# Gate and up projections of a SwiGLU: a fourth feature pair in seven products, and two pairs split by casting and adding DMAs

## The chip, the cores and the metric

The kernel runs on one core of one Trainium2 chip. The metric is the device time of one execution, in microseconds (us). The time before is 2090.59 us, the median of three runs (2089.03 to 2092.39).

## The reference

The reference is an encoder of two layers over 256 tokens of width 2048, in float32. Each layer mixes tokens (layer 0 by a gated spatial MLP, layer 1 by grouped-query attention), attends to 256 memory tokens, projects the joined heads and then runs a SwiGLU feed-forward network, which the change is about:

```
def swiglu(h, w_gate_up, w_down):
    gate, up = jnp.split(h @ w_gate_up, 2, axis=-1)
    return (jax.nn.silu(gate) * up) @ w_down

x = x + concatenate([tok_out, mem_out]) @ w_out[l]
x = x + swiglu(rms_norm(x, g_ffn[l]), w_gate_up[l], w_down[l])
```

`w_gate_up` is 2048 x 11264 (5632 gate and 5632 up columns), `w_down` 5632 x 2048.

## The kernel before, in words

Every matrix product is made of three: both operands are cut into a high part, rounded to the type float32r, and a low part, the rest, and hi x hi, lo x hi and hi x lo are accumulated in PSUM (`matmul3`, L193). The activations are cut once per layer. The weights are cut as they arrive: a DMA from SyncE's queue (SP) brings a `raw` tile of up to four 128x512 pieces, ScalarE casts it to `whi` (L248) and VectorE subtracts to get `wlo` (L249). There are three buffers each of `raw`, `whi` and `wlo` (`halves`, L244, and `W_TILES`, L35). A buffer of `whi` or `wlo` is given back when TensorE has used it; a `raw` buffer when VectorE has read it.

The feed-forward network of a layer works on 11 feature blocks of 512 gate and 512 up columns. A block is one `Pair` (L307). It walks over eight pairs of contraction chunks (2 x 128 rows each, index `i`), and each pair is a 2x2 block product: two chunks of the contraction by two token tiles on one side, two chunks by gate and up on the other. `eight` (L358) makes it in the ordinary eight products. `seven` (L340) makes it in seven, after Strassen and Winograd: VectorE first adds the four raw weight pieces to four sums `T` (L342 to L344), the three raw pieces that are used alone and the four sums are cut into halves, and the activations' sums come from `activation_sums` (L294), made once per layer for pairs 0 to 3 (`feature_sums`, L713). Of the pairs, 0, 1 and 2 are done in seven products and 3 to 7 in eight; the first block of a layer takes the five first, all the others the three first (L739).

The products land in PSUM banks by name: 1, 5, 6 and 7 in the pool `psm` (shared with all transposes), 2, 3, 4 and 8 in `psa`, four banks each. After the last pair in seven products `inner` (L367) combines 1, 5, 6 and 7 in five steps (one on ScalarE, four on VectorE), and at the block's end `outer` (L379) combines the rest in four VectorE steps. Then ScalarE takes the silu of the gate and VectorE multiplies it by up (L743, L744).

The order of the work is written in the program: `tick()` is called after every half unit of products and `later(n, fn)` puts a piece of work n ticks on. So a gate's output is transposed on TensorE and cut (`turn_a`, L731) some ticks after its block, among the products of the next one. Within the program's dependences a scheduler with a timeline model sets the order on each engine at build time; at run time each engine and each DMA queue takes its own list strictly in order.

The blocks come in chunks (L727: 4, 4 and 3 blocks). After each chunk `w_down` is applied to its outputs, in four column blocks of `Linear` (L252), and the result is added to `x` in SBUF (L753).

SBUF room: `room["p"]` is a pool that is opened for the mixing stage of a layer (36 tiles of 2 KB a partition), closed, and opened again for the feed-forward stage (24 such tiles, two `T` tiles of 8 KB, four of `e`). A new tile in it waits for the old tiles that lay in the same place. The pool `wp` (`raw`, `whi`, `wlo`) lives through the whole program.

Of the kernel before, what the change touches and what calls it, by code (L numbers as in the profile page):

```python
# [10 lines left out]
F32 = mybir.dt.float32  # L11
F32R = mybir.dt.float32r
# [21 lines left out]
FFN_TILES = 24  # L34
# [17 lines left out]
def encoder(ctx: ExitStack, tc: tile.TileContext, x, mem, g_mix, g_ffn, w_in_a, g_v_a, w_spatial, b_spatial,  # L52
# [190 lines left out]

    def halves(raw, n):  # L244

        hi = wp.tile([P, KC4, NB], F32R, tag="whi", name=nm("whi"))[:, :n]
        lo = wp.tile([P, KC4, NB], F32R, tag="wlo", name=nm("wlo"))[:, :n]
        nc.scalar.copy(hi, raw)  # L248
        nc.vector.tensor_tensor(lo, raw, hi.bitcast(F32), ALU.subtract)  # L249
        return [(hi[:, c, :], lo[:, c, :]) for c in range(n)]  # L250

    class Linear:  # L252
# [6 lines left out]
        def fetch(self, k0, n):  # L259
            raw = wp.tile([P, KC4, NB], F32, tag="raw", name=nm("raw"), bufs=3)  # L260
            src = self.w[k0 * P:(k0 + n) * P, self.n0:self.n0 + NB]
            nc.sync.dma_start(raw[:, :n], src.rearrange("(c p) n -> p c n", p=P))
            self.raw[k0] = raw
# [43 lines left out]
    class Pair:  # L307
# [3 lines left out]
        def __init__(self, parts, sums, w, na, nb, order, fast):  # L311
            self.parts, self.sums, self.w, self.na, self.nb = parts, sums, w, na, nb
            self.order, self.fast, self.bank, self.part = order, fast, {}, {}
            last = [i for i in order if i in fast][-1]
            rest = [i for i in order if i not in fast]
            for i in order:
                raw = self.fetch(i)
                (self.seven if i in fast else self.eight)(i, raw)
                if i == last:
                    self.inner()  # L320
            self.outer(bool(rest))

        def fetch(self, i):
            raw = wp.tile([P, KC4, NB], F32, tag="raw", name=nm("raw"), bufs=3)
            rows = slice(2 * i * P, (2 * i + 2) * P)
            for cut, n0 in ((slice(1, 3), self.na), (slice(0, 4, 3), self.nb)):
                nc.sync.dma_start(raw[:, cut], self.w[rows, n0:n0 + NB].rearrange("(c p) n -> p c n", p=P))
            return raw

        def add(self, name, a, b, i):  # L330
# [3 lines left out]
            some = len([x for x in self.order if x in self.fast])  # L334
            many = len(self.order) - some
            of = {1: some, 5: some, 6: some, 7: some, 8: 2 * many}.get(name, some + 2 * many)
            self.part[name] += 1
            matmul3(self.bank[name], a, b, self.part[name] == 1, self.part[name] == of)

        def seven(self, i, raw):  # L340
            T = room["p"].tile([P, KC4, NB], F32, tag="T", name=nm("T"), bufs=2)
# [11 lines left out]
            for some in (inner, outer):  # L353
                for name, a, b in some:
                    self.add(name, a, b, i)
                tick()

        def eight(self, i, raw):  # L358
            w01, w00, w10, w11 = halves(raw, 4)
            get, k0, k1 = self.parts.get, 2 * i, 2 * i + 1  # L360
            for t, names in ((0, (2, 3)), (1, (4, 8))):
                for name, pair in zip(names, ((w00, w10), (w01, w11))):
                    self.add(name, get(k0, t), pair[0], i)
                    self.add(name, get(k1, t), pair[1], i)
# [209 lines left out]
    for l in range(DEPTH):  # L574
        scope = ExitStack()
        room["p"] = scope.enter_context(tc.tile_pool(name=f"mix{l}", bufs=MIX_TILES, reuse_waits="tile"))
        cat = Parts()
        m = Memory(l)
        if l == 0:
# [28 lines left out]
            def gate(t, c):  # L608
# [4 lines left out]
                sb[t][c] = big()  # L613
# [95 lines left out]
        fast = [0, 1, 2]  # L709
        slow = [3, 4, 5, 6, 7]  # L710
        sums = {}

# [10 lines left out]
        later(4, lambda: feature_sums(1))  # L723
# [3 lines left out]
        chunks = [range(0, 4), range(4, 8), range(8, 11)]  # L727
        for chunk in chunks:
# [9 lines left out]
            for f in chunk:  # L738
                order = slow + fast if f == 0 else fast + slow  # L739
                g = Pair(hF, sums, w_gate_up[l], f * NB, DFF + f * NB, order, fast)  # L740
                for t in range(NT):
# [3 lines left out]
                    wait = 3 if f == chunk[-1] else 2 * len(fast) + 3  # L745
# [55 lines left out]
```

## Time and profile before

| what | before |
|---|---|
| median of three runs | 2090.59 us |
| the profiled execution, its own time | 2092.77 us |
| its span, first to last instruction | 2090.8 us |
| granted TensorE clock, mean | 0.991 |
| matmuls | 9346 |
| bytes moved by DMA | 396.01 MB, mean 189 GB/s |
| SP's DMA queue: packets' time as a share of 16 engines | 56.2% |

The span is shorter than the execution's own time by what lies before the first and after the last instruction. All durations in the prediction come from this one profiled execution. PE is TensorE, PEld its weight loads, DVE is VectorE, ACT ScalarE, POOL GpSimd and SP SyncE. In a group's row the first number after the bar is busy time in us, then the mean of one instruction in ns, and after the next bar the engine's idle time just before these instructions and what ended it.

### The profile page before, as it was taken

How to read it: one execution, taken by the hardware profiler on the slowest of the kernel's cores; microseconds unless marked ns; L12 is line 12 of the kernel's file. 1: busy time of each engine (PE TensorE's matmuls, PEld its weight loads, DVE VectorE, ACT ScalarE, POOL GpSimd, SP SyncE). 2: the span in 40 equal slices, each digit the busy share in tenths (PEclk: the TensorE clock that was granted, in tenths of full speed). 3: DMA queues.
4: the chain of work that ended last, by engine and by line, in shares of the span. 5: the costliest groups of instructions: out<-in, count | busy, mean ns of one | idle time of the engine just before them, and what ended most of it. 6: DMA issues, size and time to landing. Idle time of an engine off the chain costs nothing.

```text
span 2090.8 us, 23855 instructions
## 1 busy us (share of the span) xinstructions
PE 2052.3 (98%) x9346; PEld 1697.9 (81%) x9346; DVE 1485.8 (71%) x1502; ACT 1038.9 (50%) x1150; POOL 39.3 (2%) x50
## 2 busy tenths in 40 slices
PE   8799999899999999999999999998999999999999
PEld 6688888688888888888888878877888888888887
DVE  5466557987578875787567776688965889657964
ACT  7555444545344543445555654544543456434542
POOL 0010000000000000000000010000000000000000
PEclk9899999999999999999999999999999999999999
DMA  8655555465556555656556534545565655656564
GB/s 274 233 173 165 187 181 181 162 201 199 184 192 210 201 194 189 201 191 204 186 171 224 172 121 161 182 161 181 181 213 190 202 181 194 210 200 201 178 211 135
DMA packets 204696, 396.01 MB, mean 189 GB/s; under 512 B 9660, under 2 KB 12840, under 8 KB 204584
## 3 DMA queue, kind: packets, MB, share of 16 engines
q1 hardware_dynamic: 202432, 392.86, 56.2%
q10 hardware_dynamic: 2152, 1.63, 0.3%
q8 instruction: 73, 1.20, 0.2%
q14 instruction: 39, 0.32, 0.0%
HBM read 390.26 MB, written 4.19 MB: 189 GB/s over the span
## 4 chain that ended last, share of the span: by engine, by line
PE 92%; DVE 3%; issue 2%; DMA 2%; ACT 1%; SPq 0%; ACTq 0%; DVEq 0%
PE acc L195 27%; PE acc L196 27%; PE acc L197 27%; PE m L195 3%; PE m L196 3%; PE m L197 3%; PE m L201 2%; DVE wlo L249 1%; DMA a<-in_mem 1%; ACT whi L248 1%; PE m L473 0%; DVE T L342 0%; DMA gh_mq<-in_g_mq 0%; PE m L612 0%; DVE T L343 0%
## 5 line engine op out<-in xcount | busy, mean ns | idle before, releaser
L249 DVE TENSOR_TENSOR wlo<-raw,whi 128x2048 fp32r<-128x2048 f32 (+3 forms) x369 | 797.2, 2165 | 368.9 <-ACT whi L248 367.4
L248 ACT CAST whi<-raw 128x2048 fp32r<-128x2048 f32 (+3 forms) x369 | 666.5, 1812 | 646.0 <-PE acc L196 559.6
L195 PE MATMUL acc<-whi,h 128*128 128x512 f32 x1428 | 561.2, 394 | 10.1 <-DVE e L381 8.3
L196 PE MATMUL acc<-whi,h 128*128 128x512 f32 x1428 | 559.0, 392 | 0.0
L197 PE MATMUL acc<-wlo,h 128*128 128x512 f32 x1428 | 540.9, 392 | 0.0
L195 PE MATMUL acc<-whi,a 128*128 128x512 f32 x1154 | 451.5, 392 | 0.6 <-DVE a L404 0.6
L197 PE MATMUL acc<-wlo,a 128*128 128x512 f32 x1154 | 449.7, 391 | 0.0
L196 PE MATMUL acc<-whi,a 128*128 128x512 f32 x1154 | 449.5, 391 | 0.0
L195 PEld LDWEIGHTS acc<-whi,h 128*128 128x128 f32 x1428 | 270.0, 189 | 65.6 <-DVE e L381 9.1
L196 PEld LDWEIGHTS acc<-whi,h 128*128 128x128 f32 x1428 | 269.9, 189 | 55.2
L197 PEld LDWEIGHTS acc<-wlo,h 128*128 128x128 f32 x1428 | 268.7, 188 | 55.5 <-DVE wlo L249 0.4
L197 PEld LDWEIGHTS acc<-wlo,a 128*128 128x128 f32 x1154 | 217.1, 188 | 44.8
L195 PEld LDWEIGHTS acc<-whi,a 128*128 128x128 f32 x1154 | 217.2, 188 | 44.4 <-DVE a L404 0.8
L196 PEld LDWEIGHTS acc<-whi,a 128*128 128x128 f32 x1154 | 217.1, 188 | 44.0
L248 ACT CAST whi<-T 128x2048 fp32r<-128x2048 f32 x66 | 126.2, 1913 | 118.3 <-PE acc L196 110.6
L249 DVE TENSOR_TENSOR wlo<-T,whi 128x2048 fp32r<-128x2048 f32 x66 | 150.9, 2287 | 29.6 <-ACT whi L248 29.6
L342 DVE TENSOR_TENSOR T<-raw 128x1024 f32<-128x1024 f32 x66 | 80.4, 1218 | 18.7 <-DMA raw<-in_w_gate_up 18.7
L195 PE MATMUL m<-whi,a 128*128 128x512 f32 x198 | 80.0, 404 | 1.8 <-ACT whi L248 1.8
L196 PE MATMUL m<-whi,a 128*128 128x512 f32 x198 | 79.4, 401 | 0.0
L189 ACT CAST a<-m 128x512 fp32r<-128x512 f32 x80 | 46.3, 585 | 41.2 <-PE m L197 17.9
L190 DVE TENSOR_TENSOR a<-m,a 128x512 fp32r<-128x512 f32 x80 | 54.1, 684 | 17.0 <-ACT a L189 17.0
L197 PE MATMUL m<-wlo,a 128*128 128x512 f32 x198 | 55.9, 391 | 1.3 <-DVE wlo L249 1.3
(123 smaller groups left out, 1262.3 us busy)
## 6 DMA issues: line engine op xcount, KB each, us to landing
raw<-in_w_gate_up SPq DMA_DIRECT2D x352, 512.0 KB, 4.6
raw<-in_w_down SPq DMA_DIRECT2D x88, 1024.0 KB, 5.1
raw<-in_w_out SPq DMA_DIRECT2D x32, 1024.0 KB, 5.1
raw<-in_w_in_a SPq DMA_DIRECT2D x24, 1024.0 KB, 5.1
raw<-in_w_in_b SPq DMA_DIRECT2D x24, 1024.0 KB, 5.2
raw<-in_w_mem_kv SPq DMA_DIRECT2D x16, 1024.0 KB, 5.2
raw<-in_w_in_a SPq DMA_DIRECT2D x7, 512.0 KB, 5.8
x<-in_x SPq DMA_DIRECT2D x8, 256.0 KB, 4.7
```

Of the source, the lines that this page charges most:

```text
L189: nc.scalar.copy(hi, src)
L190: nc.vector.tensor_tensor(lo, src, hi.bitcast(F32), ALU.subtract)
L195: nc.tensor.matmul(out, lhsT=a[0], rhs=b[0], start=start, stop=False)
L196: nc.tensor.matmul(out, lhsT=a[1], rhs=b[0], start=False, stop=False)
L197: nc.tensor.matmul(out, lhsT=a[0], rhs=b[1], start=False, stop=stop)
L201: nc.tensor.transpose(dst[:, c * P:(c + 1) * P], src[:, c * P:(c + 1) * P], ident)
L248: nc.scalar.copy(hi, raw)
L249: nc.vector.tensor_tensor(lo, raw, hi.bitcast(F32), ALU.subtract)
L342: nc.vector.tensor_tensor(T[:, 0:2], raw[:, 1:4:2], raw[:, 0:1].to_broadcast([P, 2, NB]), ALU.add)
```

## The change

Four things are changed in the feed-forward stage:

- Pairs 0 to 3 are done in seven products, 4 to 7 in eight (before: 0 to 2, and 3 to 7). The sums for pair 3 were made before already; `feature_sums(1)` is put off from tick 4 to tick 6.
- Two of the four pairs in eight products get their halves from DMAs on GpSimd's queue (`laid`): one DMA casts the weights from float32 to float32r straight into `dhi`, ScalarE writes the negative of it into `dlo`, and a second DMA adds the weights onto that, which leaves the low half. Each of these DMAs brings 128 x 2 x 512 values (512 KB), for gate and then for up. There are three buffers each of `dhi` and `dlo`, in the pool of the feed-forward stage.
- The pairs are interleaved. In the strings F is a pair in seven products, S one in eight with halves from ScalarE and VectorE, D one in eight with halves from DMAs.
- The chunks are 3, 3, 3 and 2 blocks instead of 4, 4 and 3, and the waits before `turn_a` are set anew (15 ticks instead of 9; at the end of a chunk 3, or 1 for the chunk of two, instead of 3).

To make room, the feed-forward pool has 20 instead of 24 tiles and one `T` instead of two, `wp` has two `raw` buffers instead of three, the third one lying in the mixing stage's pool while that is open (`raw_tile`), and in layer 0 the gating result is written over `v` instead of into a tile of its own.

```
-FFN_TILES = 24
+FFN_TILES = 20
+LAID = 3
...
+    def raw_tile():
+        raws[0] += 1
+        pool = room["p"] if room["mixing"] and raws[0] % 3 == 0 else wp
+        return pool.tile([P, KC4, NB], F32, tag="raw", name=nm("raw"), bufs=1 if pool is not wp else 2)
...
+            for i, way in order:
+                if way == "D":
+                    self.laid(i)
+                else:
+                    raw = self.fetch(i)
+                    (self.seven if way == "F" else self.eight)(i, raw)
                 if i == last:
                     self.inner()
-            self.outer(bool(rest))
+            self.outer(many > 0)
+
+        def laid(self, i):
+            rows = slice(2 * i * P, (2 * i + 2) * P)
+            for n0, names in ((self.na, (2, 4)), (self.nb, (3, 8))):
+                src = self.w[rows, n0:n0 + NB].rearrange("(c p) n -> p c n", p=P)
+                hi = room["p"].tile([P, KC2, NB], F32R, tag="dhi", name=nm("dhi"), bufs=LAID)
+                lo = room["p"].tile([P, KC2, NB], F32R, tag="dlo", name=nm("dlo"), bufs=LAID)
+                nc.gpsimd.dma_start(hi, src)
+                nc.scalar.activation(lo, hi.bitcast(F32), AF.Copy, scale=-1.0)
+                nc.gpsimd.dma_start(lo, src, accum_op=ALU.add)
+                for t, name in enumerate(names):
+                    for c in range(KC2):
+                        self.add(name, self.parts.get(2 * i + c, t), (hi[:, c, :], lo[:, c, :]))
+                tick()
...
-            T = room["p"].tile([P, KC4, NB], F32, tag="T", name=nm("T"), bufs=2)
+            T = room["p"].tile([P, KC4, NB], F32, tag="T", name=nm("T"), bufs=1)
...
-                sb[t][c] = big()
+                sb[t][c] = v[t][c]
...
-        fast = [0, 1, 2]
-        slow = [3, 4, 5, 6, 7]
+        first = list(zip((4, 5, 0, 6, 1, 7, 2, 3), "DSFDFSFF"))
+        later_on = list(zip((0, 4, 1, 5, 2, 6, 3, 7), "FDFSFDFS"))
...
-        later(4, lambda: feature_sums(1))
+        later(6, lambda: feature_sums(1))
...
-        chunks = [range(0, 4), range(4, 8), range(8, 11)]
+        chunks = [range(0, 3), range(3, 6), range(6, 9), range(9, 11)]
...
-                order = slow + fast if f == 0 else fast + slow
-                g = Pair(hF, sums, w_gate_up[l], f * NB, DFF + f * NB, order, fast)
+                g = Pair(hF, sums, w_gate_up[l], f * NB, DFF + f * NB, later_on if f else first)
...
-                    wait = 3 if f == chunk[-1] else 2 * len(fast) + 3
+                    wait = 2 * len(chunk) - 3 if f == chunk[-1] else 15
```

34 lines of the change are left out of this document (17 added, 17 removed).

## The prediction

> **What bounds the kernel now.** I read the page first, then the chain of waits, the table by stretches, the list of waits, and the groups of instructions with their forms kept apart. From the page:
>
> ```profile
> span 2090.8 us, 23855 instructions
> ...
> PE 2052.3 (98%) x9346; PEld 1697.9 (81%) x9346; DVE 1485.8 (71%) x1502; ACT 1038.9 (50%) x1150; POOL 39.3 (2%) x50
> ...
> PE 92%; DVE 3%; issue 2%; DMA 2%; ACT 1%; SPq 0%; ACTq 0%; DVEq 0%
> ```
>
> TensorE carries the end: 92% of the chain that ended last is its own work. A busy figure of pipelined matmuls says little of their pace, so I take the pace from the chain in order of time, inside the gate/up stage of layer 0:
>
> ```profile
> 449.68 0.68 PE m L197 x3
> ...
> 492.10 0.68 PE m L197 x3
> ```
>
> Three matmuls of 512 columns take 0.68 us, 0.227 each (the mean of 392 ns that the page gives for one contains the overlap with the next). The two rows are the same product in neighbouring feature blocks: one block (a `Pair`, and its two gate outputs turned) takes 42.4 us. It has 3 x 7 + 5 x 8 = 61 products of three matmuls: 183 x 0.2267 = 41.5 us, and its eight transposes make up the rest. So TensorE has no hole there. The table by stretches, one such block, then the first block of layer 0:
>
> ```profile
> 437.00:479.40 42.40, 42.40 (x192) 35.12 (x192) 37.48 (x33) 22.24 (x16) 0.00 (x0) 1.00 0.59 198
> 350.00:392.00 42.00, 37.83 (x160) 30.85 (x159) 40.34 (x50) 22.09 (x20) 0.00 (x0) 0.96 0.45 150
> ```
>
> The columns are length, then PE, weight loads, VectorE (DVE), ScalarE (ACT), GpSimd (POOL) busy, granted clock, DMA share and GB/s. VectorE is busy 37.5 of 42.4 us, so it is close behind TensorE. In the first block it is the one that is late:
>
> ```profile
> PE acc L195 <- DVE e L381: 4.2, 1, 4.2
> PE m L197 <- DVE wlo L249: 1.7, 2, 1.1
> PE m L195 <- ACT whi L248: 0.7, 1, 0.7
> ```
>
> These are TensorE's waits from 340 to 410 us: 6.6 us in one layer, as three seven-product units follow each other at the block's end. So a gain comes from fewer matmuls, as long as VectorE, ScalarE and the DMAs stay ahead.
>
> **The change part by part.** Call a unit of two contraction chunks F (seven products), S (eight, split by ScalarE and VectorE) or D (eight, split by DMAs). Prices:
>
> ```profile
> L249 DVE TENSOR_TENSOR wlo<-raw,whi 128x2048 fp32r<-128x2048 f32 x294 | 671.7, 2290 | 362.6 <-ACT whi L248 362.1
> ...
> L248 ACT CAST whi<-raw 128x2048 fp32r<-128x2048 f32 x294 | 560.1, 1912 | 519.4 <-PE acc L196 448.0 <-issue 34.1 <-DMA raw<-in_w_gate_up 25.3
> ...
> L249 DVE TENSOR_TENSOR wlo<-T,whi 128x2048 fp32r<-128x2048 f32 x66 | 150.9, 2287 | 29.6 <-ACT whi L248 29.6
> L248 ACT CAST whi<-T 128x2048 fp32r<-128x2048 f32 x66 | 126.2, 1913 | 118.3 <-PE acc L196 110.6 <-DVE T L344 7.6
> L249 DVE TENSOR_TENSOR wlo<-raw,whi 128x1536 fp32r<-128x1536 f32 x66 | 115.6, 1751 | 1.4 <-ACT whi L248 0.4
> L248 ACT CAST whi<-raw 128x1536 fp32r<-128x1536 f32 x66 | 97.9, 1484 | 125.1 <-PE acc L196 111.6 <-issue 13.5
> L342 DVE TENSOR_TENSOR T<-raw 128x1024 f32<-128x1024 f32 x66 | 80.4, 1218 | 18.7 <-DMA raw<-in_w_gate_up 18.7
> ...
> L343 DVE TENSOR_TENSOR T<-T,raw 128x512 f32<-128x512 f32 x66 | 45.4, 687 | 1.2
> L344 DVE TENSOR_TENSOR T<-T,raw 128x512 f32<-128x512 f32 x66 | 45.2, 686 | 0.6
> ...
> L381 DVE TENSOR_TENSOR e<-acc,e 128x512 f32<-128x512 f32 x22 | 15.2, 690 | 57.1 <-PE acc L197 57.1
> ...
> L248 ACT CAST whi<-raw 128x1024 fp32r<-128x1024 f32 x7 | 7.3, 1048 | 1.4 <-DMA raw<-in_w_in_a 1.4
> ```
>
> *Products.* 4 x 7 + 4 x 8 = 60 instead of 61 per block: 22 blocks x 3 matmuls x 0.2267 = 15.0 us off the path itself. F lasts 21 x 0.2267 = 4.76 us on TensorE, S and D 5.44, a block 41.7.
>
> *VectorE and ScalarE.* F costs VectorE 1.218 + 0.687 + 0.686 + 1.751 + 2.287 = 6.63 us, S 2.29, D nothing. Per block one more F for an S is +4.34, two S turned to D are -4.58: -0.24, so about 37.2 of 41.7 us; still just under TensorE. ScalarE: F 3.40, S 1.91, D two negations of 128x1024. No such negation is in the trace; the cast of that size takes 1.05 and a cast of a quarter more than half of 1.91, so I take 1.05 each. That is 1.49 + 2 x 0.19 = +1.9, 24 of 41.7 us. Both are hidden by TensorE.
>
> *The order F D F S F D F S.* Before, three F in a row ask 19.9 us of VectorE in 14.3 of TensorE; now F and D ask 6.6 and F and S 8.9 in 10.2, which evens the load. Against it: the four combining steps of `inner` and, close behind, three of `outer` now lie behind the last F, with one S after it, not five. The tight place is from the moment that this F gives back its first split buffer (2.0 us into it) to the second split of the next block's first F: 2.7 + 5.4 + 0.9 (transposes) = 9.0 us. There VectorE has 1.75 + 2.29 + 7 x 0.69 = 8.9 us to do. I take no wait (VectorE idled 4.9 us in a block above, and TensorE waited for nothing); the other end is one output split more, 0.7 us late, x 22 = 15.
>
> *Raw buffers: three become two in the feed-forward stage.* Landing of a half tile (512 KB; two make a tile), as the DMA issues list it, with the spread that the view of the tensor gives:
>
> ```profile
> raw<-in_w_gate_up SPq DMA_DIRECT2D x352, 512.0 KB, 4.6
> ```
>
> ```profile
>   ACT whi L248: 25.3, 18
>   DVE T L342: 18.7, 14
> ...
> DMA to landing us min/median/max: 3.5/4.6/7.3
> ```
>
> The two upper rows are who waited for these tiles and how long; it cost TensorE nothing. The two halves are issued together, so a tile takes about 5.0. With two buffers the tightest tile is that of the next block's first F: its buffer is free when the last F's first split is done (3.2 us after the split buffer, which is free with the fourth unit at 20.4 us of the block): 23.6 + 5.0 + 2.6 for T = 31.2, and its own split buffer is free at 32.6. So 1.4 us of room before a late landing reaches VectorE. I take 0.
>
> *D units.* Each D is four 512 KB DMAs on GpSimd's queue (8 a block, 176 in all): cast into hi, negate on ScalarE, add into lo, for gate and then for up. GpSimd's queue is otherwise empty here (0.00 above). What queues behind the waits: the adding DMA waits for the negation and holds the next cast DMA on that queue; the negation waits for the cast DMA and holds ScalarE's casts behind it. No row shows a casting or adding DMA. Near end: two landings of 4.6 + 1.05 = 10.3 us; far end: the slowest row twice, 2 x 7.3 + 1.05 = 15.7. With three buffers each of hi and lo, the shortest stretch from release to use is from the middle of one D to the middle of the next: 2.72 + 4.76 + 5.44 + 4.76 + 2.72 = 20.4. Both ends fit, so I take 0; landings over (20.4 - 1.05)/2 = 9.7 do not fit.
>
> *The first D of each layer.* Now the layer starts with a D whose tiles lie where the mixing stage's pool lay. How early loading ran ahead before, and where TensorE's work starts:
>
> ```profile
> 313.55 29.59 SPq L327 DMA_DIRECT2D raw<-in_w_gate_up  x12
> ```
>
> ```profile
> 337.42 0.39 PE L195 MATMUL acc<-whi,h 128*128 128x512 f32 x1
> ```
>
> Raw tiles had their own pool and could start 24 us ahead. The D tiles wait for the mixing tiles under them, some of which the output projection may read to its end: 0 (all free 10 us ahead) to 10.3 us (none). I take 2 per layer, nearer the low end since only lo's place can be that late and it is wanted 4.6 us after hi's.
>
> *One more chunk end (3+3+3+2 for 4+4+3).* The same down products, eight more accumulations into x per layer on VectorE, which has room in the down stage; TensorE waits at no chunk end now. The last block of the two-block chunk is turned after one step of 2.7 us, when its gate is ready by the combining steps above: 0, at most 1 per layer. `sb` in place, pool sizes and the third raw tile in the mixing pool keep three raw tiles there: 0.
>
> *First block of a layer.* D S F D F S F F ends in S F F instead of F F F; the 6.6 us of waits may shrink or, with `inner` still behind the last F, stay: I take 0.
>
> Sum: the profiled run's own 2092.77 - 15.0 + 2 x 2 = 2081.8; the median of the three runs, 2090.59, lies 2.2 below it: **2079.6**. With the first D between 0 and 2 x 4.6 and up to 6 us fewer first-block waits, this case lies between 2069 and 2086.
>
> **The rivals.**
>
> *Late landings (slower).* Place: the raw tile of the next block's first F. Now 8 MB a block are read at a DMA share of 0.59; then it is 10 MB, 0.59 x 10/8 x 42.4/41.7 = 0.75, with adding DMAs at the price of plain ones. It decides when a tile takes over 6.4 us; each us beyond costs up to 1 x 22. For it: VectorE and ScalarE waited for these tiles even with three buffers. Against it: 0.75 leaves room. At 7.5 us a tile: 2079.6 + 1.1 x 22 = 2104. The Trainium skill, "Collectives: The Full Stack", section on the bandwidth ceiling, states that an add in the DMA engines is slow because it reads two sources; by that the share would be 0.59 x 12/8 x 42.4/41.7 = 0.90, and this rival is the likelier; no run here shows it yet.
>
> *Late D chain (slower).* As above, from 9.7 us a landing; two short stretches a block, 44 in all, each 0.1 us more costs 0.2 x 44 = 9; at 10.2 us 2079.6 + 44 = 2124. Twice the median row is only 9.2.
>
> *The gain is eaten at the layers' starts (same).* The lo tiles lie under mixing tiles that are read to the end: 1.05 + 4.6 = 5.7, up to 10.3 us per layer: 2079.6 - 4 + 11 to 21, about 2090.
>
> *More than the products (faster).* The even order also ends the first blocks' waits and the first D is early: 2090.6 - 15.0 - 13.2 = 2062.
>
> **How the numbers follow.** A measurement of this kernel can tell 0.2%, 4.2 us, from no change. Forecast 0.45, more than that 0.10, eaten 0.15, late landings 0.22, late chain 0.08. Faster: 0.45 + 0.10 = 0.55; same 0.15; slower 0.30. The range leaves out the lower half of the faster rival and the late chain with the worst of the late landings: 2066 to 2112.
>
> **What would show it.** In the profile after: 66 x 3 = 198 matmuls fewer; the same product 41.7 us apart in neighbouring blocks; VectorE near 37 us in each; DMA share near 0.75; GpSimd's DMAs landing in under 9.7 us; TensorE's waits in a layer's first unit of a few us. A TensorE wait for D tiles or for raw in every block, or a block longer than 42.4 us, would prove the forecast wrong.

## The result: slower by 3.5%, and the profile after

The changed kernel takes 2165.27 us (median of 4 runs, 2162.83 to 2166.82) where the kernel before took 2091.34 beside it: ratio 1.035, interval 1.034 to 1.037. That is 74 us slower where 11 us faster was forecast. The profiled execution has a span of 2161.9 us, 71.1 above that of before. The page of the changed kernel:

```profile
span 2161.9 us, 24106 instructions
...
PE 2061.1 (95%) x9280; PEld 1690.4 (78%) x9280; DVE 1495.2 (69%) x1562; ACT 1072.3 (50%) x1216; POOL 211.6 (10%) x226
...
PE 56%; issue 25%; DMA 6%; DVE 5%; POOL 4%; ACT 3%; POOLq 0%; SPq 0%; ACTq 0%; DVEq 0%
```

There are 66 matmuls fewer (9346 to 9280), which at 0.2267 us are the 15.0 us of the forecast. But TensorE's share of the chain that ended last fell from 92% to 56%: the end is now set by a chain that leaves TensorE again and again. VectorE's total hardly moved. So 71.1 + 15.0 = 86.1 us came from somewhere else, and the list of TensorE's waits is the first place to look. After (who waited for whom: us in total, times, longest):

```profile
PE m L196 <- ACT whi L257: 26.1, 22, 2.7
PE acc L198 <- DMA dlo<-in_w_gate_up: 21.7, 2, 11.4
PE acc L196 <- ACT whi L257: 14.6, 10, 4.0
...
PE acc L196 <- DVE e L409: 7.7, 6, 2.2
```

The 14 rows of this list add up to 96.7 us; the 10 rows of the same list of the kernel before add up to 34.4. Two things are new: two waits of 10 to 11 us, one a layer, for a D tile's low half, and 32 waits for a cast of ScalarE, 40.7 us in all, where before there were three. Beside waits there is pace. The granted clock was 0.991 over 2090.8 us before; after:

```profile
core 0: 2161.9 us, clock 0.983
```

Taken as time lost, (1 - clock) x span, that is 18.8 us before and 36.8 after. The account is then 62.3 us of waits and up to 18.0 of clock, at most 80.3 of 86.1. The two overlap: in the first row below the clock is low while TensorE has four matmuls to do, and 12 x (1 - 0.66) = 4.1 us are counted on both sides. The rest is not placed. (The clock's part is an estimate from these figures.) Where the clock falls is seen in the table by stretches of the changed kernel (length, PE, weight loads, DVE, ACT, POOL busy, clock, DMA share, GB/s):

```profile
342.00:354.00 12.00, 0.61 (x4) 0.19 (x2) 10.67 (x25) 6.85 (x11) 6.24 (x6) 0.66 0.72 161
354.00:390.00 36.00, 35.78 (x144) 28.71 (x144) 17.01 (x20) 14.80 (x12) 7.75 (x8) 0.92 0.80 203
609.30:651.40 42.10, 42.10 (x191) 34.81 (x190) 35.57 (x34) 24.07 (x20) 7.77 (x8) 1.00 0.88 241
651.40:695.90 44.50, 40.59 (x175) 32.53 (x174) 33.55 (x32) 21.65 (x17) 7.79 (x8) 0.96 0.78 217
684.00:688.00 4.00, 4.00 (x12) 3.10 (x12) 4.00 (x2) 2.97 (x3) 0.00 (x0) 0.60 0.55 209
```

The first two rows are a layer's first D: 12 us with four matmuls in them, then a lower clock. The third row is a block that runs nearly as forecast, 42.1 us for 41.7. The fourth is the last block of the same chunk, 44.5 us, and the fifth four microseconds of it, behind a wait.

**The first D.** GpSimd's instructions of the changed kernel around the start of layer 0's gate/up stage (start, us, instruction, the idle time before it and what ended it):

```profile
326.12 2.38 POOL L346 DMA_DIRECT2D dhi<-in_w_gate_up  x3 [169.76 <-DVE h L224]
340.05 0.55 POOL L180 TENSOR_SCALAR s<-s 128x1 f32<-128x1 f32 x1 [11.55 <-DVE s L242]
...
343.60 1.15 POOL L183 TENSOR_TENSOR s<-s,mhalf 128x1 f32<-128x1 f32 x1
344.71 2.49 POOL L348 DMA_DIRECT2D dlo<-in_w_gate_up  x2
```

ScalarE in the same stretch, its first negation and the wait before the work in front of it:

```profile
338.01 0.63 ACT L205 ACTIVATE junk<-x 128x512 f32<-128x512 f32 x1 [3.57 <-DVE x L596]
...
340.29 1.05 ACT L347 ACTIVATE dlo<-dhi 128x1024 fp32r<-128x1024 f32 x1
```

The casting DMAs went out at 326 us, early enough. The negation ran only at 340.29, behind ScalarE's part of the norm, which had waited for the mixing stage's result; whether the place of the low half was free earlier does not show. The adding DMA could then have gone out at 341.3. It went out at 344.7, 3.4 us later: on GpSimd's in-order queue it stands behind the four small operations of the norm (L180, L183), which wait 11.6 us for the sum of squares of the same result. It landed 9.2 us after its issue. TensorE waited 11.4 us for the first low half and got it at 353.9. So GpSimd's queue accounts for 3.4 us of the wait, the late negation and the landing for the rest.

**The last block of a chunk.** The same kernel, several engines, 662 to 685 us. The raw tiles are those of an S unit (subtracted at 662.36), of a unit of seven (W at 667.75) and of the next unit of seven (cast at 675.74):

```profile
662.36 2.28 DVE L258 TENSOR_TENSOR wlo<-raw,whi 128x2048 fp32r<-128x2048 f32 x1
...
667.75 1.76 DVE L258 TENSOR_TENSOR wlo<-raw,whi 128x1536 fp32r<-128x1536 f32 x1 [0.27 <-ACT whi L257]
...
670.14 0.69 DVE L372 TENSOR_TENSOR T<-T,raw 128x512 f32<-128x512 f32 x1
...
675.74 1.48 ACT L257 CAST whi<-raw 128x1536 fp32r<-128x1536 f32 x1 [2.88 <-DMA raw<-in_w_gate_up]
...
678.92 1.22 DVE L370 TENSOR_TENSOR T<-raw 128x1024 f32<-128x1024 f32 x1
...
681.70 1.90 ACT L257 CAST whi<-T 128x2048 fp32r<-128x2048 f32 x1 [4.49 <-DVE T L372]
...
683.65 0.69 PE L196 MATMUL m<-whi,a 128*128 128x512 f32 x1 [2.70 <-ACT whi L257]
684.14 0.63 PE L197 MATMUL m<-whi,a 128*128 128x512 f32 x1
684.57 0.63 PE L196 MATMUL m<-whi,a 128*128 128x512 f32 x1
```

SyncE's queue from 664 to 668 us and from 669 to 676:

```profile
664.67 0.92 SPq L358 DMA_DIRECT2D raw<-in_w_gate_up  x2
```

```profile
670.90 0.97 SPq L358 DMA_DIRECT2D raw<-in_w_gate_up  x2
```

How long the two halves of the first pair took, then all gate/up raw loads of the changed kernel:

```profile
DMA to landing us min/median/max: 7.2/8.9/10.6
```

```profile
DMA to landing us min/median/max: 3.6/5.3/11.3
```

Read it from below. TensorE waits 2.70 us for the cast of T, the cast 4.49 for T's last addition, which comes after a W split, whose cast waited 2.88 for the raw tile. With two buffers that tile takes the place of the S unit's, so it was asked for when the S unit's subtraction had ended, at 664.67; its second half landed at 675.64, 10.6 us after that half's issue. (The pair at 670.90 is the tile after it, which waited for the third T addition of the unit of seven between, until 670.83.) With three buffers it would take the place of the tile before the S unit's, whose last reader had ended when the loads at 658.17 went out: 6.5 us earlier, an estimate, since the order would shift too. So two things meet in this chain: a request held back by the second buffer, and a landing of twice the usual time.

Landings were longer in general. The halves' median rose only from 4.6 to 5.3 us, but their longest from 7.3 to 11.3, and a tile needs both halves. From the first issue to the second landing, where the trace's records have both, a tile took 5.1 us in the median before (132 tiles) and 6.6 after (102 tiles); over 6.4 us were 12 of them before and 55 after.

After TensorE's wait matmuls start every 0.43 us, twice the usual 0.227, for some 4 us. T's last addition now often gives a raw buffer back last, as the queue that issues the loads shows, after:

```profile
SPq L358 <- DVE wlo L258: 434.0, 75, 27.2
SPq L358 <- DVE T L372: 418.1, 54, 11.7
```

and before, where T's additions almost never came last:

```profile
SPq L327 <- DVE T L344: 29.5, 4, 7.8
```

The transfers themselves, after (GpSimd's queue with packets, MB and share of 16 engines' time; then issues, KB, median us to landing):

```profile
q0 software_dynamic: 47872, 92.29, 20.1%
...
dhi<-in_w_gate_up POOLq DMA_DIRECT2D x88, 512.0 KB, 5.3
dlo<-in_w_gate_up POOLq DMA_DIRECT2D x88, 512.0 KB, 7.8
```

### The profile page after: what moved, and what is told of

It is laid out like the page before. It is cut to its first block, busy times and chain, and to the rows that moved or that the text cites. A ratio compares the mean times of both kernels' runs of the same rounds, so it can differ in the third digit from the quotient of the medians.

```text
span 2161.9 us, 24106 instructions
## 1 busy us (share of the span) xinstructions
PE 2061.1 (95%) x9280; PEld 1690.4 (78%) x9280; DVE 1495.2 (69%) x1562; ACT 1072.3 (50%) x1216; POOL 211.6 (10%) x226
## 3 DMA queue, kind: packets, MB, share of 16 engines
q0 software_dynamic: 47872, 92.29, 20.1%
## 4 chain that ended last, share of the span: by engine, by line
PE 56%; issue 25%; DMA 6%; DVE 5%; POOL 4%; ACT 3%; POOLq 0%; SPq 0%; ACTq 0%; DVEq 0%
PE acc L198 16%; PE acc L196 16%; PE acc L197 16%; DVE wlo L258 3%; DMA raw<-in_w_down 3%; ACT whi L257 3%; POOL dlo L348 2%; PE m L196 2%; PE m L197 2%; PE m L198 2%; POOL dhi L346 1%; PE m L202 1%; DMA raw<-in_w_gate_up 1%; DMA dhi<-in_w_gate_up 1%; DMA a<-in_mem 1%
## 5 line engine op out<-in xcount | busy, mean ns | idle before, releaser
L258 DVE TENSOR_TENSOR wlo<-raw,whi 128x2048 fp32r<-128x2048 f32 (+3 forms) x325 | 686.2, 2112 | 355.2 <-ACT whi L257 354.0
L257 ACT CAST whi<-raw 128x2048 fp32r<-128x2048 f32 (+3 forms) x325 | 573.9, 1766 | 435.9 <-PE acc L197 264.1
L196 PE MATMUL acc<-whi,a 128*128 128x512 f32 x1176 | 461.5, 394 | 11.3 <-ACT whi L257 7.9
L196 PE MATMUL acc<-whi,h 128*128 128x512 f32 x944 | 374.6, 398 | 11.6 <-ACT whi L257 6.7
L197 PE MATMUL acc<-whi,h 128*128 128x512 f32 x944 | 372.8, 395 | 0.0
L198 PE MATMUL acc<-wlo,h 128*128 128x512 f32 x944 | 356.6, 395 | 0.6 <-DVE wlo L258 0.6
L196 PEld LDWEIGHTS acc<-whi,a 128*128 128x128 f32 x1176 | 221.8, 189 | 59.6 <-ACT whi L257 10.9
L196 PEld LDWEIGHTS acc<-whi,h 128*128 128x128 f32 x944 | 180.4, 191 | 52.0 <-ACT whi L257 7.4
L198 PEld LDWEIGHTS acc<-wlo,h 128*128 128x128 f32 x944 | 179.3, 190 | 38.7 <-DVE wlo L258 1.4
L197 PEld LDWEIGHTS acc<-whi,h 128*128 128x128 f32 x944 | 180.3, 191 | 36.8
L347 ACT ACTIVATE dlo<-dhi 128x1024 fp32r<-128x1024 f32 x88 | 92.9, 1059 | 136.1 <-DMA dhi<-in_w_gate_up 100.4
L198 PE MATMUL acc<-dlo,h 128*128 128x512 f32 x352 | 137.2, 397 | 21.7 <-DMA dlo<-in_w_gate_up 21.7
L196 PE MATMUL acc<-dhi,h 128*128 128x512 f32 x352 | 139.0, 395 | 0.0
L197 PE MATMUL acc<-dhi,h 128*128 128x512 f32 x352 | 138.7, 394 | 0.0
L348 POOL DMA_DIRECT2D dlo<-in_w_gate_up x88 | 106.0, 1222 | 294.4 <-ACT dlo L347 264.0
```

The source lines that it names most:

```text
L196: nc.tensor.matmul(out, lhsT=a[0], rhs=b[0], start=start, stop=False)
L197: nc.tensor.matmul(out, lhsT=a[1], rhs=b[0], start=False, stop=False)
L198: nc.tensor.matmul(out, lhsT=a[0], rhs=b[1], start=False, stop=stop)
L347: nc.scalar.activation(lo, hi.bitcast(F32), AF.Copy, scale=-1.0)
L348: nc.gpsimd.dma_start(lo, src, accum_op=ALU.add)
```

## The experiments

Three theories stood at the start. **Buffers**: the room for the D tiles was made by giving up a raw and a T buffer, and the loss is the lead lost with them. **DMAs**: the adding transfers are dear, and make loads or D tiles late. **Order and load**: four units of seven spread through a block are more than VectorE can follow. The kernel before took 2089 to 2094 us (medians) beside these runs; ratios are to it, and where two runs are compared, it is by their distances to it.

**1. The price of the adding DMAs.** The changed kernel with an add of 32 of 512 columns, and with a second cast instead of the add:

```diff
-                nc.gpsimd.dma_start(lo, src, accum_op=ALU.add)
+                nc.gpsimd.dma_start(lo[:, :, :32], src[:, :, :32], accum_op=ALU.add)   # e2_add_small
+                nc.gpsimd.dma_start(lo, src)                                           # e3_add_plain
```

> The change with the adding DMA cut to 32 of 512 columns of each piece, so that it keeps its place, its wait and its issue on GpSimd's queue but brings a sixteenth of the bytes (the low halves are left wrong for the other columns). Theory late landings: the adding DMAs fill the DMA engines, the raw tiles land late, and the waits in every chunk's third block (32 us in six) and at the start of the down stages (13 us) vanish, part of the first-D wait too: 2105 to 2120 us, DMA share of a block near 0.67 instead of 0.82. Rival buffers: two raw tiles and one T leave no lead whatever the traffic: 2150 or more. Rival order: inner and outer behind the last F: 2150 or more too.

> The change with the second DMA not adding but only casting the same bytes into dlo (the low halves are then wrong). It parts the price of the add from the price of the bytes. If an adding DMA costs the DMA engines twice a plain one (software queue 20.1% of the time for 92.29 MB, 0.218% per MB, against 0.138 on SP's queue), the share of a block falls from 0.82 to about 0.75 and the time to about 2130 to 2145; if the add itself is free, 2160 or more.

Measured: 2141.7 us (1.023, 1.020 to 1.026) and 2146.2 (1.025, 1.021 to 1.029). So 48 of the 74 us stay when the add is all but gone: DMAs as the main cause fall, but they are a part, as the first time lies between its two forecasts. With the small add TensorE's two waits for the first D fell from 21.7 to 12.7 us in all, and the raw tiles land almost as before: 5.2 us a tile in the median, and of the halves (all gate/up raw loads)

```profile
DMA to landing us min/median/max: 3.6/4.6/7.9
```

TensorE's waits for casts fell only from 40.7 to 29.8 us. The run with the second cast also gives the price of the add by itself:

```profile
q0 software_dynamic: 47872, 92.29, 15.0%
...
dlo<-in_w_gate_up POOLq DMA_DIRECT2D x88, 512.0 KB, 5.4
```

A casting transfer of this size lands in 5.4 us, an adding one in 7.8. Half of 15.0 is 7.5 points for one set of casts; 20.1 - 7.5 = 12.6 points for the adds, 1.7 times as much.

The Trainium skill, "Collectives: The Full Stack", section on the bandwidth ceiling, has the add reading two sources; 1.7 for 2 agrees in direction, and the DMA share of one block (0.88 above, with 0.78 in the next) came near the 0.90 that it gave. The time hung on it in part: 26 of the 74 us went with the add.

**2. The two buffers, taken from the kernel before.** Two raw buffers in the feed-forward stage (the third in the mixing pool, as the change has it), and by itself one T buffer:

```diff
-            raw = wp.tile([P, KC4, NB], F32, tag="raw", name=nm("raw"), bufs=3)
+            raw = raw_tile()                                                         # e4_before_raw2
-            T = room["p"].tile([P, KC4, NB], F32, tag="T", name=nm("T"), bufs=2)
+            T = room["p"].tile([P, KC4, NB], F32, tag="T", name=nm("T"), bufs=1)     # e7_before_T1
```

> The kernel before with two raw buffers in the feed-forward stage and the third in the mixing stage's pool, nothing else. Theory late landings: two buffers are enough at the traffic of before: 2090 to 2098 us. Rival buffers: the lost lead is most of the loss: 2115 or more.

> The kernel before with one T buffer instead of two, nothing else. Theory buffers holds for raw alone or for T too: if one T costs much of it here too, with three F in a row, 2105 or more; if only raw does, 2092 to 2097 us.

Measured: 2147.9 us (1.026, 1.022 to 1.029) and 2200.0 (1.052, 1.049 to 1.055). In a kernel with no D and no DMA on GpSimd one raw buffer less costs 54 us, one T buffer less 108. TensorE's first waits with two raw buffers:

```profile
PE m L195 <- ACT whi L256: 22.8, 21, 1.7
PE m L197 <- DVE wlo L257: 19.9, 32, 1.6
```

and with one T buffer:

```profile
PE m L195 <- ACT whi L248: 52.0, 36, 4.5
```

Both are in the higher of the two ranges expected. In the run with two raw buffers no half took over 6.2 us to land, so that loss needs no late landing. The second loss is larger; a likely reason is that three units of seven follow each other there, and each must wait until the one before has split its T.

**3. Giving them back in the changed kernel.** There is no room for two T, three raw and three D buffers at once with chunks of three blocks. So one is paid for with another:

```diff
-LAID = 3
+LAID = 2
-        pool = room["p"] if room["mixing"] and raws[0] % 3 == 0 else wp
-        return pool.tile([P, KC4, NB], F32, tag="raw", name=nm("raw"), bufs=1 if pool is not wp else 2)
+        return wp.tile([P, KC4, NB], F32, tag="raw", name=nm("raw"), bufs=3)         # e5_raw3_laid2
-            T = room["p"].tile([P, KC4, NB], F32, tag="T", name=nm("T"), bufs=1)
+            T = room["p"].tile([P, KC4, NB], F32, tag="T", name=nm("T"), bufs=2)     # e9_T2_laid2
```

(the last two lines and LAID = 2 in the second run, whose raw buffers stay two)

> The change with three raw buffers in a pool of their own again, as before, paid for by two instead of three buffers each of dhi and dlo. Theory buffers: with two raw tiles the next tile's load cannot start until the last one is read, and that lost lead is what costs TensorE its waits in third blocks (32 us), at the start of the down stages (16) and after the layer change (8): 2165 - 45 to 55 = 2110 to 2120 us, the first-D waits staying. Rival D chain: D's DMAs (landing 5.3 and 7.8 us) are what is late; two buffers make the shortest stretch 17.7 instead of 20.4 us and it gets worse: 2165 or more.

> The changed kernel with two T buffers again, paid for with two buffers each for the D tiles' hi and lo instead of three; raw buffers stay two. Lost buffers (T above all): VectorE no longer stops about 2 us in each unit of seven between the T additions and the second subtraction, so most of the waits inside the blocks go, what is left is the raw tile and the first D of each layer: 2105 to 2130. D chain or traffic: the D tiles have less lead than before, so it stays at 2150 or above.

Measured: 2150.6 us (1.028, 1.025 to 1.032) and 2179.3 (1.042, 1.038 to 1.046): both far above what the buffer theory said. TensorE's waits show why. Three raw buffers, two for the D tiles:

```profile
PE acc L198 <- DMA dlo<-in_w_gate_up: 52.2, 29, 11.1
...
PE m L196 <- ACT whi L256: 6.3, 7, 2.1
...
PE acc L196 <- ACT whi L256: 2.0, 1, 2.0
```

With two T buffers and two for the D tiles the first row is 52.5 us, 32 times.

With three raw buffers the waits for ScalarE's casts go (26.1 and 14.6 us to 6.3 and 2.0), as the theory says, and waits for D tiles come instead, in both runs: the chain of cast, negation and add, 5.3 + 1.06 + 7.8 = 14.2 us, starts when the half two before has been used, not the half three before. The buffers were needed in both places.

**4. Two T and three raw buffers, in smaller chunks.** Chunks of 2+2+2+2+2+1 leave room for both with two D buffers; the second run has three units of seven a block instead of four. In both a chunk of one block turns its gate's output at once:

```diff
-FFN_TILES = 20
+FFN_TILES = 16
-        chunks = [range(0, 3), range(3, 6), range(6, 9), range(9, 11)]
+        chunks = [range(k, min(k + 2, 11)) for k in range(0, 11, 2)]                 # e10_T2_raw3
...
-        first = list(zip((4, 5, 0, 6, 1, 7, 2, 3), "DSFDFSFF"))
-        later_on = list(zip((0, 4, 1, 5, 2, 6, 3, 7), "FDFSFDFS"))
+        first = list(zip((4, 5, 0, 6, 1, 7, 2, 3), "DSFDSSFF"))
+        later_on = list(zip((0, 4, 1, 5, 2, 6, 3, 7), "FDFSFDSS"))                   # e11_three_F_two_D
```

> The changed kernel with the two T buffers and the three raw buffers of the kernel before, two buffers for the D tiles, and chunks of 2+2+2+2+2+1 blocks to make the room (16 more accumulations of 0.7 us per layer on VectorE in the down stages). Lost buffers: the blocks run at the pace of their products again; the 15 us of products show, less the first D of each layer (10 to 14 us each): 2090 to 2108. D chain or traffic: blocks stay slow, 2130 or above.

> As the kernel with two T and three raw buffers and chunks of two, but only three units of seven a block, in the order F D F S F D S S: the D part alone, without the fourth seven. VectorE's load falls by 4.3 us a block. Lost buffers: only the first D of each layer costs, 2105 to 2120 (15 us of products not gained); if VectorE's load with four sevens is what makes the blocks late, this one is nearer to the kernel before than the one with four is to its own product pace. D chain or traffic: 2130 or above.

Measured: 2171.4 us (1.038, 1.030 to 1.046), and 2130.9 (1.019, 1.016 to 1.021): both misses for the buffer theory, the second by 11 us. In the run with three sevens the D units cost next to nothing after a layer's first block. TensorE's waits for low halves there are six in all, four of them in the two first blocks (28.0 of 28.6 us), the longest the first of a layer:

```profile
PE acc L198 <- DMA dlo<-in_w_gate_up: 28.6, 6, 11.1
```

So two D buffers do when VectorE has one seven less; with four they don't. In the run with four, the waits for D tiles (20.3 us, 15 times) are joined by waits for the turning and combining steps on VectorE (18.8 us, 17 times, and 10.7, 8 times).

**5. The fourth seven by itself.** Order F S F S F S F S (S S F S F S F F in a layer's first block), no D, all buffers and chunks of before:

```diff
-        later_on = list(zip((0, 4, 1, 5, 2, 6, 3, 7), "FDFSFDFS"))
+        later_on = list(zip((0, 4, 1, 5, 2, 6, 3, 7), "FSFSFSFS"))                   # e12_four_F_no_D
```

> The fourth seven alone: order F S F S F S F S, no D, chunks of 4+4+3, and all buffers of the kernel before (three raw, two T). VectorE then has about 26.5 + 9.2 + 6.2 = 41.9 us of work in a block of 41.7 us of products, so without any D the kernel is at VectorE's limit. Lost buffers: 2078 to 2095, since no buffer is given up and there is no first D. If four sevens spread through a block are themselves what VectorE can't follow: over 2100.

Measured: 2118.0 us (1.012, 1.009 to 1.015). Two stretches of it, about a block each:

```profile
658.00:706.00 48.00, 44.92 (x192) 35.32 (x192) 44.26 (x39) 23.28 (x18) 0.00 (x0) 0.98 0.54 180
706.00:751.00 45.00, 43.67 (x191) 35.13 (x191) 41.52 (x37) 23.48 (x18) 0.00 (x0) 0.98 0.54 185
```

VectorE is busy 44.3 of 48 us and 41.5 of 45, 42.9 in the mean, where the products of a block take 41.7: here it is the bound, so the fourth seven can't be had without taking two S from VectorE. That part of the change's arithmetic was sound.

**6. VectorE's load and ScalarE's queue in the changed kernel.** The S units without their subtraction; and the negations on GpSimd:

```diff
-            w01, w00, w10, w11 = halves(raw, 4)
+            hi = wp.tile([P, KC4, NB], F32R, tag="whi", name=nm("whi"))
+            nc.scalar.copy(hi, raw)
+            w01, w00, w10, w11 = [(hi[:, c, :], hi[:, c, :]) for c in range(4)]      # e15_no_S_sub
...
-                nc.scalar.activation(lo, hi.bitcast(F32), AF.Copy, scale=-1.0)
+                nc.gpsimd.tensor_scalar(lo, hi.bitcast(F32), -1.0, None, ALU.mult)   # e13_negate_gpsimd
```

> The changed kernel without the subtraction that makes the low halves of the S units (their high halves are used in place of the low ones, so the result is only roughly the reference's there): VectorE has 4.6 us less to do in a block, while products, buffers, D tiles and DMAs stay. VectorE's load as the cause: the waits in the blocks go but for the first D, 2110 to 2135. D chain, DMA traffic or lost raw buffers as the cause: 2150 or more.

> The changed kernel with the negations of the D units on GpSimd instead of ScalarE, so that ScalarE's casts are no longer queued behind a wait for a casting DMA. If ScalarE held by the negations is what makes the third block of a chunk late: 2125 to 2145. If it is VectorE's load and its lost buffers: 2155 or more (a longer chain of the first D if GpSimd negates more slowly).

(The second asks of a later theory, that ScalarE's casts wait behind the negations in its queue.) Measured: 2146.8 us (1.026, 1.023 to 1.029) and 2185.1 (1.045, 1.041 to 1.048). Taking 4.6 us a block from VectorE, 101 us in all, wins 19, between the two forecasts: its load by itself is not the main cause. TensorE's waits for casts fell from 40.7 to 15.3 us there, but 18.4 us of waits for the turning steps on VectorE (L191) came in place. For ScalarE's queue the other run does not decide. TensorE's waits for casts fell from 40.7 to 26.3 us, but on GpSimd the negation takes three times as long, and TensorE waits for D tiles 14 times, 25.3 us in all, in later blocks too:

```profile
L347 POOL TENSOR_SCALAR dlo<-dhi 128x1024 fp32r<-128x1024 f32 x88 | 289.6, 3295 | 153.8 <-DMA dhi<-in_w_gate_up 118.2 <-PE acc L198 15.8 <-issue 5.8
```

That the casts do queue behind waiting negations is seen in ScalarE's row of the changed kernel; what it costs TensorE stays open:

```profile
ACT dlo L347 <- DMA dhi<-in_w_gate_up: 100.4, 45, 8.7
```

**7. The first block of a layer.** The order alone, in the changed kernel and in the one before:

```diff
-        first = list(zip((4, 5, 0, 6, 1, 7, 2, 3), "DSFDFSFF"))
+        first = list(zip((4, 5, 0, 6, 1, 7, 2, 3), "SSFDFDFF"))                      # e1_first_ssf
...
-                order = slow + fast if f == 0 else fast + slow
+                order = fast + slow if f else [3, 4, 0, 5, 1, 6, 2, 7]               # e8_before_first
```

> The change with the order of a layer's first block alone altered, D S F D F S F F to S S F D F D F F, so that the first D comes third of a kind, 16 us later. Theory: TensorE's two waits for dlo at the layers' starts (21.7 us in all in the changed kernel, and slowed matmuls behind each) come only from the D chain starting when the mixing pool is let go; then they vanish: 2135 to 2143 us against 2165. Rival: the chain is simply too slow in a first block, and the wait moves to the later D: 2155 or more.

> The kernel before with only a layer's first block reordered: S S F S F S F S instead of S S S S S F F F. If the first block's waits (12.6 and 13.6 us over the plain pace in a layer's first two blocks) come from three F in a row at its end, followed by three more, most of them go: 2070 to 2084 us against 2092. If they come from the work that a layer's start brings with it (norms, the activations' sums), they stay or move ahead: 2090 or more.

Measured: 2151.5 us (1.028, 1.025 to 1.031), 16 us less, the waits for low halves down from 21.7 us in two to 12.9 in five, so the wait moved in part; and 2090.6 (1.000, 0.999 to 1.001). So in the kernel before, spreading the sevens of the first block changes nothing. The changed order also in the run with three raw and two D buffers of part 3:

> The same with the first block of a layer as S S F D F D F F. Theory buffers, with the first-D wait a separate loss of 14 us or a little more: 2090 to 2105 us, so the change comes back to the time of before but gains little beyond it. Rival D chain: 2150 or more.

Measured: 2158.7 (1.032, 1.029 to 1.036) for 2150.6 without it, no gain there.

**8. Chunks, raw buffers and the first D, one after another.** First chunks of two alone; then three raw buffers beside three D buffers, for which these chunks leave room (T stays one); then also the first block of a layer without D:

```diff
-        chunks = [range(0, 3), range(3, 6), range(6, 9), range(9, 11)]
+        chunks = [range(k, min(k + 2, 11)) for k in range(0, 11, 2)]                 # e16_chunks_of_two
...
-        pool = room["p"] if room["mixing"] and raws[0] % 3 == 0 else wp
-        return pool.tile([P, KC4, NB], F32, tag="raw", name=nm("raw"), bufs=1 if pool is not wp else 2)
+        return wp.tile([P, KC4, NB], F32, tag="raw", name=nm("raw"), bufs=3)         # e17_two_raw3
...
-        first = list(zip((4, 5, 0, 6, 1, 7, 2, 3), "DSFDFSFF"))
+        first = list(zip((3, 4, 5, 6, 7, 0, 1, 2), "SSSSSFFF"))                      # e18_two_raw3_first
```

> The changed kernel with chunks of 2+2+2+2+2+1 blocks for 3+3+3+2, nothing else. If VectorE loses lead from block to block and wins it back in the down stage: the 32 us that the third blocks lose go, 2125 to 2145. If the loss belongs to each end of a chunk or to the D units: the same or more, 2160 to 2185.

> The kernel with chunks of 2+2+2+2+2+1 and one T buffer and three buffers for the D tiles, now with three raw buffers as in the kernel before. If the two raw buffers make the down products' first tiles late: TensorE's waits there go (about 75 us of the 2207), the first D of each layer stays: 2115 to 2135. If it is the single T buffer or the D units at each chunk's end: 2170 or more.

> The same with the first block of each layer in the order of the kernel before (S S S S S F F F, no D, 61 products in it). If raw buffers and the first D are the whole loss, the first blocks cost about 13 us a layer as before and the later blocks run at the pace of 60 products: 2085 to 2105, with 20 x 0.68 = 13.6 us of products gained against one T buffer's and one more chunk end's cost. If the single T buffer costs on its own in the later blocks: 2120 or more.

Measured: 2206.9 us (1.055, 1.050 to 1.060), 2146.1 (1.027, 1.025 to 1.030) and 2135.6 (1.022, 1.021 to 1.024). The first is the opposite of what "lead lost from block to block" expects: the chunks' ends cost. TensorE waits there for the first tiles of the down products, and ScalarE for their raw tiles. Chunks of two, two raw buffers, TensorE's row and ScalarE's:

```profile
PE acc L196 <- ACT whi L257: 54.9, 12, 6.7
```

```profile
ACT whi L257 <- DMA raw<-in_w_down: 106.9, 38, 5.7
```

A tile of these is used up in 24 matmuls of 0.227, 5.4 us, about what a load takes by itself (a median of 5.1 in the changed kernel), and cast and subtraction come on top. The third raw buffer alone brings 58 us (115.1 over the kernel before become 57.4); ScalarE's row falls to 4.5 us, once, and TensorE's to 2.3. What is left with three:

```profile
PE acc L198 <- DMA dlo<-in_w_gate_up: 19.9, 3, 10.8
PE acc L196 <- DVE e L409: 15.5, 9, 3.2
```

and with no D in the first block:

```profile
PE acc L196 <- DVE e L409: 15.8, 10, 2.5
PE m L196 <- ACT whi L256: 11.7, 8, 3.5
PE m L202 <- DVE sg L772: 11.6, 2, 5.8
```

The first row of the last fence but one is the first D of each layer; without it the time falls by 10.5 us, though the two first blocks have one product more each (1.4 us). Still the best of these is 47 us over the kernel before, and its expectation of 2085 to 2105 missed; what it named for a cost of the one T, 2120 or more, is where it lies. The three rows of the last fence name 39 us: the combining steps behind the last F, which hold the accumulator that the next stage's first product needs, a cast behind the one T, and the chunk of a single block, which is these chunks' own.

An attempt with everything that had helped apart from each other, two T, three raw and two D buffers, negations on GpSimd and no D in the first block:

> Two T and three raw buffers, two buffers for the D tiles, chunks of two, the negations on GpSimd, and the first block of each layer as in the kernel before (S S S S S F F F, no D; 61 products in it). ScalarE's queue as the cause: every block but the first of a layer at the pace of its products, 2080 to 2100. VectorE's load as the cause: the blocks stay 1 to 5 us late each, 2115 to 2145. In both cases the first blocks cost as in the kernel before, about 13 us a layer.

Measured: 2164.4 us (1.035, 1.027 to 1.042), TensorE waiting 32.3 us for low halves, 22 times: the slow negation and the two D buffers again. No version that was run is faster than the kernel before by more than a measurement can tell.

## Why the prediction was wrong, point by point

*Products.* Right: 15.0 us, 66 matmuls. (The line on what would show it said 198; it multiplied by three twice. The sum did not.)

*VectorE and ScalarE.* VectorE's work in an undisturbed block (35.6 of 42.1 us) is no larger than before, and a negation takes 1.06 us for the 1.05 assumed. Hidden by TensorE, as said, as long as their inputs are there; less load on VectorE alone won 19 us.

*Raw buffers: three become two.* This is the step that failed. "1.4 us of room", so 0. Four errors are in it, and the chain above shows three of them. The buffer was taken as free when W of the unit before is split; T's third addition reads it after that (670.83 for 669.5). The new tile's T was taken to follow the landing at once; it comes 3.3 us after it, behind the cast and most of the subtraction of the new W (675.64 and 678.92). A tile was taken to land in about 5.0 us; the two in that chain took 11.0 and 7.5 from first issue to second landing, and the median was 6.6. And only the gate/up blocks were looked at: the down products, a tile every 5.4 us, run on the same buffers. Measured: 54 us in the kernel before, 58 in the changed one with chunks of two. In the changed kernel as it is, a third raw buffer took away 32.4 of the 40.7 us of waits for casts; its price in time there is not known, since two D buffers paid for it.

*One T buffer.* It had no price at all; the order's arithmetic treated T as made ahead. In the kernel before it costs 108 us with three sevens in a row. How much of that the spread order saves was not measured by itself, since two T, three raw and three D buffers do not fit together. Open.

*D units.* 0 was right for TensorE's own waits with three buffers: the median landings of 5.3 and 7.8 us are under the 9.7 that the sum allowed, and the later blocks show no wait for D tiles. What the sum named and did not price, ScalarE's casts held behind a negation, happened (100.4 us of ScalarE's time); its cost is open. The chain of one half, 14.2 us, lies inside the bounds of 10.3 and 15.7. With two buffers TensorE waits 52 us for it.

*The first D of each layer.* 2 us forecast, 10.9 measured (21.7 for both layers), just outside the bounds' far end of 10.3, and a lower clock behind it. (The range took 2 x 4.6 for the two layers, less than that far end; by these terms the case's upper bound is 2084.8, not 2086.) The reason given, tiles under the mixing stage's, is not borne out for the high half, whose casting DMA was early, and not decided for the low half. What shows is a chain that the sum lacked: the negation ran only behind the norm's work on ScalarE (340.29), then "GpSimd's queue is otherwise empty", read from a block inside the stage, did not hold at the layer's start, where the norm's small operations hold the adding DMA 3.4 us, and that DMA took 9.2 us, twice the 4.6 assumed.

*Order.* "I take no wait", other end 15 us for combining steps in front of a split. In the changed kernel TensorE waited 7.7 us for them, 6 times; with three raw buffers and chunks of two 15.5 and 15.8 us, the far end.

*A further chunk end.* 0 to 1 forecast. With two raw buffers each chunk end costs; two more a layer cost 41 us in all.

*The rivals.* "Late landings" happened, as a part: 55 of 102 tiles took over the 6.4 us from which it was to decide, and 26 us went with the adds, some of them the first D's. It is not the main cause: 48 us stay without it, and two raw buffers cost 54 in the kernel before, where landings were short. "Late D chain" needed landings over 9.7; TensorE waited for no D tile after the first. "The gain is eaten at the layers' starts" happened, for 22 us and clock. The range's upper end, 2112, was made of one rival at a time; three of the causes came together.

*Clock.* No term of the sum held it. Up to 18 us of the loss are lower clock, part of it inside the waits and the rest what they leave behind.

## What to carry to other kernels

Room for a new tile has a price: before giving up a buffer, write out the whole loop that it closes, last reader, load, every step up to the product, in the order in which the engines really do them, for each stage that uses the buffer, and compare it with the products between two uses. Take the landing of the whole tile under the new traffic for the load, not the median of its parts under the old. Price each buffer by itself in the old kernel; here two runs of that kind would have told more than the whole sum. And when a DMA is issued from an engine's queue, look at what stands in that queue, and in the queue of the engine that it waits for, at every place where the DMA will be, not in the middle of a steady stage.

## What was not expected of the hardware

**Half pace after short waits.** A TensorE wait of 2.70 us is followed by matmuls 0.43 us apart for about 4 us (clock 0.60 in that stretch); an 11.4 us wait by a clock of 0.92 over the next 36 us. Many short waits mostly do not do it: with four sevens and no D TensorE's listed waits are 58.5 us, all but three of them under 2 us, and the granted clock is 0.993. In the changed kernel's trace all twelve waits of over 2.2 us after the kernel's start have a stretch of half clock during or just behind them, and of the fifteen between 0.9 and 1.9 us one has. So the same sum of waits costs more in long pieces; the wait of 2.70 us cost 4 x (1 - 0.60) = 1.6 us on top, an estimate from the stretch's row.

The Trainium skill, "TensorE: Matmul & The Clock Gate", section "What's actually happening", says that the array falls to half clock after an idle window of about 3.4 us; the trace agrees on the half pace and shows it behind a gap of under 3 us.

**The add in a DMA** takes 7.8 us to land where a cast takes 5.4, and 1.7 times the engines' time; a negation of 128x1024 takes 1.06 us on ScalarE and 3.30 on GpSimd.
